# Seven block products for two of the mixer's column groups, in a four-layer decoder trunk

## The chip, the core and the metric

The kernel runs on one core of a Trainium2 chip. The metric is the device time of one execution in microseconds (us). The engines are TensorE (PE, with its weight loads as PEld), VectorE (DVE), ScalarE (ACT), GpSimd (POOL) and SyncE (SP), which issues the transfers from HBM. Each works through its own queue in order and waits for the others through semaphores.

## The reference

Four residual layers work on x of 256 tokens x 1024 features, all in float32:

```
for i in range(4):
    hn   = rmsnorm(x, g_mix[i])
    proj = hn @ w_in[i]                   # 1024 -> 3*1024 + 256
    cols, mq = proj[:, :3072], proj[:, 3072:]
    mix  = stick_breaking(cols)           # layers 1 and 4: q, k, v
         | diff_attention(cols, ...)      # layer 2:        q, k, v
         | b * conv3(c * h)               # layer 3:        b, c, h
    mo   = memory_attention(mq, rmsnorm(mem), w_mem_kv[i])
    x    = x + concat(mix, mo) @ w_o[i]
    x    = x + (silu(g) * u) @ w_ffn_out[i]   where g, u = rmsnorm(x) @ w_ffn_in[i]
out = rmsnorm(x, g_final)
```

The three 1024-wide parts of the mixer's projection are queries, keys and values in layers 1, 2 and 4, and the gates b, c and the input h in layer 3. The feed-forward part is 2816 wide.

## The kernel before

The tokens are two tiles of 128 (t = 0, 1); the 1024 features are eight chunks of 128 (kc). Every weight is split on the core into a high part that TensorE multiplies in its fast float32 form and a low part, weight minus high part; activations are split likewise. A product of activations and weights is then three matmuls (`mm3`, L135 to L138): high x high, high x low, low x high. `wparts` (L128) makes the two parts: a cast on ScalarE (`whi`, L131) and a subtraction on VectorE (`wlo`, L132), each for a chunk of 128 x 1024 numbers.

`proj` (L157) multiplies the tokens by one group of 512 weight columns: four chunks of two kc each, then, for each tile t, 8 x 3 matmuls of 128 x 512 into one PSUM bank, and an output function `evac(t, ps)`. The mixer works on two halves g = 0, 1 of the features: `mixer(g)` calls `proj` for 512 columns of q, of k and of v (in layer 3 of c, of h and of b). The transposes of the outputs, the attention and the convolution are put on a list with `later(n, f)` and are traced n flushes later; `proj` flushes in the middle and at the end of each token tile. So the small work of one group comes between the matmuls of the next ones. `memory()` (L716) projects the memory queries, 256 columns, and puts the cross-attention on the list.

`strassen` (L197) is a second way to do two column groups at once. It treats the tokens as a 2 x 2 matrix of blocks (token tile x half of the features) and the weights of the two groups as another (half of the features x group) and forms the product from seven block products instead of eight (Winograd's variant of Strassen's scheme). The products run in the order 1, 5, 7, 6 (each in two steps s of 256 features, the four of s = 0 before those of s = 1), then 2, 4 and 3. Their 14 weight chunks are made by eight sums of weight blocks on VectorE (`plus`, L224, 128 x 1024 each) and 14 calls of `wparts`. The sums `su` and `sy` of finished products are formed on VectorE, and `out(t, side, ps, add)` receives each of the four output blocks, three of them with an addition. Each of the seven products is 4 x 3 matmuls. `tokens_side` (L269) forms the sums of token blocks from the transposed inputs `xg`: four additions and four subtractions of 128 x 512 on VectorE, four casts on ScalarE. One group of outputs comes with its sign reversed, and `negative(rx)` gives the scale that puts it right.

Before the change the feed-forward part uses `strassen` for its column groups b = 1 and b = 4 (gate and up columns together), and straight `proj` calls for the other groups. `tokens_side` stands behind the first `proj` of b = 0.

The raw weights come from HBM on the SP queue into a pool of eight buffers (`wraw`), which also holds the weight sums. The parts stand in eight buffers each (`wsplit`). The output projection (`out_proj`, L293) keeps its last four chunks in `wsplit` until its end, where each of its four PSUM banks is finished in turn and handed to the residual addition, the norm's statistics and the transposes for the next stage. The transposed inputs `xg` stand in four buffers named `qkn`, which other work uses too; the split token blocks stand in a pool of eleven buffers named `att`.

Order on each engine: the kernel doesn't write it out. Instructions are traced in program order, and a planner puts them on the engines' queues by that order and by what is ready at its own reckoning, waiting for buffers where a pool is full. On the chip each queue is then strictly in order.

Of the kernel before, what the change touches and what calls it, by code (L numbers as in the profile page):

```python
# [9 lines left out]
F32 = mybir.dt.float32  # L10
# [7 lines left out]
P = 128  # L18
# [22 lines left out]
def trunk_kernel(ctx, tc, x, mem, vecs, w_in, w_kv, w_o, w_f1, w_f2, lams, g_final, out):  # L41
# [101 lines left out]
    def later(rounds, f):  # L143
        pend.append([rounds, f])
# [320 lines left out]
    def qkv_evac(dst, scale):  # L465
        def evac(t, ps):
            n = work.tile([P, 512], F32, name="qkn", tag="qkn", bufs=4)
            nc.scalar.activation(n, ps, AF.Copy, scale=scale[t])
            later(1, lambda: to_T(n, dst[:, :, t * P:(t + 1) * P], 1))
        return evac  # L470
# [231 lines left out]


    kv = None
    for i in range(DEPTH):
        kind = i % 3
        col = lambda c, n=512: [w_in[i, :, c:c + n]]
# [8 lines left out]
        def memory():  # L716
            mqT = big.tile([P, 2, 2, S], F32R, name="mqT", tag="big")

            def evac(t, ps):
                n = work.tile([P, MEMW], F32, name="mk", tag="att", bufs=NATT)  # L720
                nc.scalar.activation(n, ps[:, :MEMW], AF.Copy, scale=rx[t])
                later(1, lambda: queries(t, n))

            def queries(t, n):
                tr = ps_x.tile([P, 4, P], F32, name="tr", tag="ps")
                for c in range(2):
                    nc.tensor.transpose(tr[:, c, :], n[:, c * P:(c + 1) * P], ident)
                split(mqT, tr[:, :2, :], t)

            proj(col(3 * D, MEMW), xT, evac)  # L730
            later(2, lambda: om.append(mem_attention(mqT, kv)))

        rq = []

        def q_scale(t):
            r = small.tile([P, 1], F32, name="rq", tag="sm", bufs=14)
            nc.vector.tensor_scalar(r, rx[t], QSCALE, None, ALU.mult)
            return r
# [5 lines left out]
        if kind != 2:  # L744
            v = [big.tile([P, D], F32, name=f"v{t}", tag="big") for t in range(NT)]

            def mixer(g):
                qT = big.tile([P, 4, S], F32, name="qT", tag="big")
                kT = big.tile([P, 4, S], F32, name="kT", tag="big")
                sc = []  # L750

                def q_evac(t, ps):
                    if g == 0:
                        rq.append(q_scale(t))
                    qkv_evac(qT, rq)(t, ps)

                def scores():
                    if kind == 0:
                        sb_scores(qT, kT, sc, values)
                    else:  # L760
                        diff_scores(qT, kT, 2 * g, lam, sc, values)

                def v_evac(t, ps):
                    nc.scalar.activation(v[t][:, g * 512:(g + 1) * 512], ps, AF.Copy, scale=rx[t])

                def values():
                    outputs(g)
                    if kind == 0:
                        sb_values(sc, v, g * 512, oh[g], ol[g])
                    else:  # L770
                        diff_values(sc, v, g * 512, oh[g], ol[g], ghead)

                proj(col(g * 512), xT, q_evac, second_tile if i == 0 and g == 0 else None)
                if i > 0 and g == 0:
                    memory()
                if i == 0 and g == 0:
                    fetch_mem()
                proj(col(D + g * 512), xT, qkv_evac(kT, rx))
                if i == 0 and g == 0:
                    load_mem()  # L780
                later(2, scores)
                proj(col(2 * D + g * 512), xT, v_evac)
        else:
            def mixer(g):
                cn = [work.tile([P, 512], F32, name="cn", tag="qkn", bufs=4) for _ in range(NT)]
                uT = big.tile([P, 4, S], F32, name="uT", tag="big")
                bT = big.tile([P, 4, S], F32, name="bT", tag="big")

                def c_evac(t, ps):
                    nc.scalar.activation(cn[t], ps, AF.Copy, scale=rx[t])  # L790

                def h_evac(t, ps):
                    nc.vector.scalar_tensor_tensor(cn[t], ps, rx[t], cn[t], ALU.mult, ALU.mult)
                    later(1, lambda: to_T(cn[t], uT[:, :, t * P:(t + 1) * P], 1))

                def mix():
                    outputs(g)
                    conv_mix(bT, uT, oh[g], ol[g], g)

                proj(col(D + g * 512), xT, c_evac)  # L800
                if g == 0:
                    memory()
                proj(col(2 * D + g * 512), xT, h_evac)
                proj(col(g * 512), xT, qkv_evac(bT, rx))
                later(2, mix)

        mixer(0)
# [89 lines left out]
        def f_lhs(kc, t):  # L897
# [1 line left out]
            sl = slice(t * P, (t + 1) * P)  # L899
            return hh[:, kc % 4, sl], hl[:, kc % 4, sl]  # L900

        nxt, rnx = [], []
        out_proj(w_f2[i], list(range(NFF // 2)), f_lhs, 2,
                 residual(V_MIX + 8 * (i + 1), nxt, rnx) if i + 1 < DEPTH else final())
        xT, rx = nxt, rnx


# [28 lines left out]
```

## Time and profile before

| what | value |
|---|---|
| median of 3 runs | 1285.72 us (1285.38 to 1285.79) |
| the profiled execution | 1284.95 us |
| its span, first to last instruction | 1283.2 us |
| granted TensorE clock | 0.998 |
| busy: PE, PEld, DVE, ACT, POOL | 99%, 82%, 72%, 56%, 4% |
| weights read from HBM | 225 MB, 176 GB/s over the span |

Busy times are unions of the profiled instructions. Matmuls overlap one another, so the duration of one is longer than the distance between the starts of two, and a busy TensorE is not TensorE at its peak. A row of a group gives its count, its busy time and the mean duration of one; a row of waits gives the sum, the count and the longest. In a timeline the first two numbers are start and duration in us, and the bracket gives the idle time before the instruction and what ended it. Layers are counted from 1 in this text and from 0 in the code (i).

### The profile page before, as it was taken

What the parts mean: (1) busy time and instruction counts of PE and PEld (TensorE: products, weight loads), DVE (VectorE), ACT (ScalarE), POOL (GpSimd) and SP (SyncE); (2) the same over time, 40 slices, a digit from 0 to 9 for tenths busy, and PEclk for the clock granted to TensorE, in tenths of its full rate; (3) what the DMA queues carried; (4) which work ended last, traced back from release to release, by engine and by line L of the source; (5) the groups of instructions that cost most, each with busy time, mean ns of one, the idle gap of its engine ahead of it and who ended that gap; (6) DMA issues with size and microseconds to landing.
All of it is one profiled execution on the core that took longest, in us unless ns stands there. A gap on an engine that the chain in (4) does not pass through costs nothing.

```text
span 1283.2 us, 16324 instructions
## 1 busy us (share of the span) xinstructions
PE 1270.3 (99%) x6079; PEld 1046.2 (82%) x6079; DVE 923.2 (72%) x1147; ACT 721.4 (56%) x1015; POOL 55.0 (4%) x109
## 2 busy tenths in 40 slices
PE   9999999999999999999999999999999999999997
PEld 6888888878888888887888888887888888888786
DVE  7755599884566769988466778988646656998942
ACT  7756466564455646656355455656436755665642
POOL 1000000000111000000000000000000001000001
PEclk9999999999999999999999999999999999999999
DMA  9644438386554344848655553666765444383840
GB/s 347 199 145 134 145 115 279 116 290 206 149 184 131 132 148 122 272 131 291 191 158 164 173 190 105 200 202 200 244 195 165 132 132 148 103 279 110 270 156 33
DMA packets 107791, 227.34 MB, mean 177 GB/s; under 512 B 7488, under 2 KB 20288, under 8 KB 107712
## 3 DMA queue, kind: packets, MB, share of 16 engines
q1 hardware_dynamic: 107712, 226.31, 55.1%
q8 instruction: 47, 0.77, 0.2%
q14 instruction: 32, 0.26, 0.1%
HBM read 225.23 MB, written 1.05 MB: 176 GB/s over the span
## 4 chain that ended last, share of the span: by engine, by line
PE 91%; DVE 5%; ACT 1%; DMA 1%; issue 1%; SPq 0%; POOL 0%; POOLq 0%; ACTq 0%
PE acc L136 25%; PE acc L138 25%; PE acc L137 25%; PE acc L214 3%; DVE wlo L132 3%; PE acc L215 3%; PE acc L216 3%; PE tr L864 1%; PE tr L361 1%; PE tr L347 1%; DVE wsum L224 1%; ACT whi L131 1%; PE tr L430 1%; DMA raw<-in_w_ffn_out 1%; PE at L411 1%
## 5 line engine op out<-in xcount | busy, mean ns | idle before, releaser
L132 DVE TENSOR_TENSOR wlo<-raw,whi 128x1024 fp32r<-128x1024 f32 (+1 forms) x428 | 512.5, 1210 | 202.0 <-ACT whi L131 199.6
L131 ACT CAST whi<-raw 128x1024 fp32r<-128x1024 f32 (+1 forms) x428 | 438.8, 1042 | 291.0 <-PE acc L138 215.1
L136 PE MATMUL acc<-whi,xth 128*128 128x512 f32 (+1 forms) x896 | 353.5, 395 | 0.1
L137 PE MATMUL acc<-wlo,xth 128*128 128x512 f32 (+1 forms) x896 | 342.8, 383 | 1.6 <-DVE wlo L132 1.6
L138 PE MATMUL acc<-whi,xtl 128*128 128x512 f32 (+1 forms) x896 | 343.8, 384 | 0.0
L138 PEld LDWEIGHTS acc<-whi,xtl 128*128 128x128 f32 x896 | 168.4, 188 | 33.8
L137 PEld LDWEIGHTS acc<-wlo,xth 128*128 128x128 f32 x896 | 168.9, 188 | 32.6 <-DVE wlo L132 2.8
L136 PEld LDWEIGHTS acc<-whi,xth 128*128 128x128 f32 x896 | 168.6, 188 | 31.5 <-issue 0.8
L136 PE MATMUL acc<-whi,hh 128*128 128x512 f32 x320 | 125.4, 392 | 0.0
L138 PE MATMUL acc<-whi,hl 128*128 128x512 f32 x320 | 124.6, 389 | 0.0
L137 PE MATMUL acc<-wlo,hh 128*128 128x512 f32 x320 | 124.6, 389 | 0.0
L131 ACT CAST whi<-wsum 128x1024 fp32r<-128x1024 f32 x48 | 50.5, 1052 | 42.7 <-DVE wsum L224 39.2
L138 PEld LDWEIGHTS acc<-whi,hl 128*128 128x128 f32 x320 | 60.1, 188 | 12.6
L137 PEld LDWEIGHTS acc<-wlo,hh 128*128 128x128 f32 x320 | 60.1, 188 | 12.2
L136 PEld LDWEIGHTS acc<-whi,hh 128*128 128x128 f32 x320 | 60.1, 188 | 12.1
L132 DVE TENSOR_TENSOR wlo<-wsum,whi 128x1024 fp32r<-128x1024 f32 x48 | 58.4, 1217 | 5.8 <-ACT whi L131 5.2
L136 PE MATMUL acc<-whi,oh 128*128 128x512 f32 x128 | 51.1, 399 | 0.0
L214 PE MATMUL acc<-whi,sh 128*128 128x512 f32 x128 | 51.0, 399 | 0.0
L138 PE MATMUL acc<-whi,ol 128*128 128x512 f32 x128 | 50.0, 391 | 0.0
L216 PE MATMUL acc<-whi,sl 128*128 128x512 f32 x128 | 50.0, 390 | 0.0
L215 PE MATMUL acc<-wlo,sh 128*128 128x512 f32 x128 | 49.9, 390 | 0.0
L137 PE MATMUL acc<-wlo,oh 128*128 128x512 f32 x128 | 49.9, 390 | 0.0
(219 smaller groups left out, 1563.8 us busy)
## 6 DMA issues: line engine op xcount, KB each, us to landing
raw<-in_w_ffn_in SPq DMA_DIRECT2D x160, 512.0 KB, 4.5
raw<-in_w_in SPq DMA_DIRECT2D x100, 512.0 KB, 4.4
raw<-in_w_ffn_out SPq DMA_DIRECT2D x88, 512.0 KB, 4.6
raw<-in_w_o SPq DMA_DIRECT2D x40, 512.0 KB, 4.2
raw<-in_w_mem_kv SPq DMA_DIRECT2D x16, 512.0 KB, 4.4
raw<-in_w_ffn_in SPq DMA_DIRECT2D x32, 256.0 KB, 3.1
raw<-in_w_in SPq DMA_DIRECT2D x8, 256.0 KB, 5.6
x<-in_x SPq DMA_DIRECT2D x4, 256.0 KB, 4.2
```

Source lines behind the costliest of these rows:

```text
L131: nc.scalar.copy(hi, raw)
L132: wlast[:] = [nc.vector.tensor_tensor(lo, raw, hi.bitcast(F32), ALU.subtract)]
L136: nc.tensor.matmul(ps, lh, wh, start=first, stop=False)
L137: nc.tensor.matmul(ps, lh, wl, start=False, stop=False)
L138: return nc.tensor.matmul(ps, ll, wh, start=False, stop=last)
L214: nc.tensor.matmul(acc[b], lh[:, kc, :], w[0][:, k, :], start=start, stop=False, skip_group_check=True)
L215: nc.tensor.matmul(acc[b], lh[:, kc, :], w[1][:, k, :], start=False, stop=False, skip_group_check=True)
L216: nc.tensor.matmul(acc[b], ll[:, kc, :], w[0][:, k, :], start=False, stop=stop, skip_group_check=True)
L224: nc.vector.tensor_tensor(out, a, b, ALU.add)
L347: last_pe = nc.tensor.transpose(ps[:, c, :], src[:, kc * P:(kc + 1) * P], ident).ins
L361: nc.tensor.transpose(ps[:, c, :], src[:, c * P:(c + 1) * P], ident)
L411: nc.tensor.matmul(pss[r][:, pr, :], qT[r * 64:(r + 1) * 64, a, pr, t * P:(t + 1) * P], kT[r * 64:(r + 1) * 64, b, pr, :], start=a + b == ...
```

## The change

In layers 2 to 4 (i > 0) the first half (g = 0) of the mixer no longer does its three groups by three `proj` calls. In layers 2 and 4 the values' group comes first, by `proj`; queries and keys follow together by `strassen`; the memory queries come behind them, and the scores are put on the list ahead of the memory queries. In layer 3 the gate b comes first, then c and h by `strassen`, then the memory queries. The outputs go through `qk_out` (scale and transpose) and `ch_out` (scale, product, transpose). To feed `tokens_side`, the transposed inputs of the mixer are kept from the feed-forward part before (`xg_in`), and `tokens_later` puts `tokens_side` on the list, two flushes into the first `proj`. The second half g = 1 and layer 1 stay as they were.

```
+    xg_in = None
...
+        def tokens_later(xg=xg_in):
+            got = []
+            later(2, lambda: got.append(tokens_side(xg, xT)))
+            return got
...
+                def qk_out(t, side, ps, add):
+                    n = work.tile([P, 512], F32, name="qkn", tag="qkn", bufs=4)
+                    if add is not None:
+                        nc.vector.tensor_tensor(n, ps, add, ALU.add)
+                    nc.scalar.activation(n, ps if add is None else n, AF.Copy, scale=(rneg if side else rq)[t])
+                    later(1, lambda: to_T(n, (kT if side else qT)[:, :, t * P:(t + 1) * P], 1))
...
+                if i > 0 and g == 0:
+                    side = tokens_later()
+                    proj(col(2 * D), xT, v_evac)
+                    rq.extend(q_scale(t) for t in range(NT))
+                    rneg = negative(rx)
+                    strassen(col(0)[0], col(D)[0], side[0], qk_out)
+                    later(2, scores)
+                    memory()
+                    return
+
                 proj(col(g * 512), xT, q_evac, second_tile if i == 0 and g == 0 else None)
-                if i > 0 and g == 0:
-                    memory()
...
+                def ch_out(t, side, ps, add, got={}):
+                    src = ps
+                    if add is not None:
+                        src = cn[t] if side == 0 else add
+                        if (t, side) == (0, 1):
+                            src = work.tile([P, 512], F32, name="sx", tag="att", bufs=NATT)
+                        nc.vector.tensor_tensor(src, ps, add, ALU.add)
+                    if side == 0:
+                        nc.scalar.activation(cn[t], src, AF.Copy, scale=rx[t])
+                    got[t, side] = src
+                    if (t, 1 - side) in got:
+                        nc.vector.scalar_tensor_tensor(cn[t], got[t, 1], rneg[t], cn[t], ALU.mult, ALU.mult)
+                        later(1, lambda: to_T(cn[t], uT[:, :, t * P:(t + 1) * P], 1))
...
-                proj(col(D + g * 512), xT, c_evac)
                 if g == 0:
+                    side = tokens_later()
+                    proj(col(0), xT, qkv_evac(bT, rx))
+                    rneg = negative(rx)
+                    strassen(col(D)[0], col(2 * D)[0], side[0], ch_out)
                     memory()
-                proj(col(2 * D + g * 512), xT, h_evac)
-                proj(col(g * 512), xT, qkv_evac(bT, rx))
+                else:
+                    proj(col(D + g * 512), xT, c_evac)
+                    proj(col(2 * D + g * 512), xT, h_evac)
+                    proj(col(g * 512), xT, qkv_evac(bT, rx))
                 later(2, mix)
...
-        nxt, rnx = [], []
+        nxt, rnx, xg_in = [], [], []
         out_proj(w_f2[i], list(range(NFF // 2)), f_lhs, 2,
-                 residual(V_MIX + 8 * (i + 1), nxt, rnx) if i + 1 < DEPTH else final())
+                 residual(V_MIX + 8 * (i + 1), nxt, rnx, xg_in) if i + 1 < DEPTH else final())
```

## The prediction

> **What bounds the kernel now.** I read the head of the page first, then the chain that ended last, then who makes TensorE wait.
>
> ```profile
> span 1283.2 us, 16324 instructions
> PE 1270.3 (99%) x6079; PEld 1046.2 (82%) x6079; DVE 923.2 (72%) x1147; ACT 721.4 (56%) x1015; POOL 55.0 (4%) x109
> PE 91%; DVE 5%; ACT 1%; DMA 1%; issue 1%; SPq 0%; POOL 0%; POOLq 0%; ACTq 0%
> PE acc L214 <- DVE sy L224: 2.5, 4, 0.7
> PEld acc L214 <- DVE sy L224: 5.3, 8, 1.1
> ```
>
> TensorE is never idle for long and carries 91% of the chain, so a matmul taken away is worth its price as long as the other engines keep up. The only wait of TensorE that comes back in every layer lies inside the seven-product block itself (L214), which the kernel already uses twice in each feed-forward part. VectorE at 72% is an average, and the stages will turn out to differ.
>
> The price of a matmul is not its duration in the groups (0.39 us), since matmuls overlap. It is the distance from start to start. TensorE's timeline in the second feed-forward output projection:
>
> ```profile
> 299.78 0.39 PE L136 MATMUL acc<-whi,hh 128*128 128x512 f32 x1
> ...
> 336.95 0.39 PE L138 MATMUL acc<-whi,hb 128*128 128x512 f32 x1
> 337.19 0.60 PE L347 MATMUL tr<-ident,x 128*128 128x128 f32 x4
> 337.54 0.48 PE L136 MATMUL acc<-whi,hh 128*128 128x512 f32 x1
> ```
>
> From the first to the second row lie 164 steps: 37.17 / 164 = 0.2267 us a matmul. A group of four transposes takes 337.54 - 337.19 = 0.35 us.
>
> Now the stages of one layer by window (columns: length, busy time of each engine, clock, share of the DMA engines, GB/s):
>
> ```profile
> core 0: us, PE busy (x) PEld busy (x) DVE busy (x) ACT busy (x) POOL busy (x), PEclk, DMA share, GB/s
> 479.90:502.80 22.90, 22.90 (x108) 18.95 (x107) 22.41 (x29) 16.12 (x22) 0.75 (x2) 1.00 0.42 120
> 502.80:522.60 19.80, 19.80 (x89) 15.99 (x88) 19.77 (x22) 13.56 (x16) 0.00 (x0) 1.00 0.62 187
> 662.60:674.10 11.50, 11.50 (x56) 9.52 (x55) 9.70 (x13) 8.30 (x11) 1.82 (x2) 1.00 0.66 189
> 355.90:362.20 6.30, 6.30 (x55) 6.30 (x54) 3.33 (x4) 3.14 (x4) 0.00 (x0) 1.00 0.86 294
> 662.60:745.50 82.90, 82.47 (x431) 67.49 (x430) 62.62 (x104) 44.99 (x70) 1.82 (x2) 1.00 0.54 166
> ```
>
> The first row is the feed-forward part's first pair of column groups, done straight (two `proj`); the second is its next pair, done as seven products. The pair costs 22.9 less two transpose groups, 22.2 us; the seven products cost 19.8 less one, 19.45 us. So the same trick saves 2.7 us in a place where the trace shows it. But in both rows VectorE is full: 22.41 of 22.9 and 19.77 of 19.8. There the block has two straight projections ahead of it in which VectorE can run ahead. In the changed mixer it has one. That is the question of this change.
>
> **The change, part by part.** *Matmuls.* Two straight groups are 2 x 48 matmuls of 128x512, seven products are 7 x 4 x 3 = 84. Twelve fewer in each of three layers, 12 x 0.2267 = 2.72 us a layer, 8.2 us in all, all of it on the path. Transposes, memory queries (48 matmuls of 256 columns, the 6.30 us row) and weight transfers stay the same in number. The page "TensorE: Matmul & The Clock Gate" of the Trainium skill (section "Wait — 56ns, not 53.3ns?") puts warm 512-column matmuls 215.7 ns apart; this trace has 226.7. By the page the 36 matmuls would be 7.8 us, an estimate; the row decides.
>
> *VectorE.* Prices from its timeline:
>
> ```profile
> 333.03 1.23 DVE L132 TENSOR_TENSOR wlo<-raw,whi 128x1024 fp32r<-128x1024 f32 x1 [1.50 <-ACT whi L131]
> ...
> 342.86 1.23 DVE L132 TENSOR_TENSOR wlo<-raw,whi 128x1024 fp32r<-128x1024 f32 x1 [0.98 <-ACT whi L131]
> 344.00 0.68 DVE L355 TENSOR_TENSOR xtl<-xg,xth 128x512 fp32r<-128x512 f32 x1
> 344.61 0.68 DVE L351 TENSOR_TENSOR xg<-tr,vec 128x512 f32<-128x512 f32 x1
> ...
> 349.92 0.99 DVE L355 TENSOR_TENSOR xtl<-xg,xth 128x512 fp32r<-128x512 f32 x1
> ...
> 470.29 1.22 DVE L224 TENSOR_TENSOR wsum<-raw 128x1024 f32<-128x1024 f32 x1
> 472.21 1.23 DVE L224 TENSOR_TENSOR raw<-raw 128x1024 f32<-128x1024 f32 x1
> ...
> 488.26 1.22 DVE L224 TENSOR_TENSOR wsum<-raw 128x1024 f32<-128x1024 f32 x1
> ...
> 498.81 1.21 DVE L132 TENSOR_TENSOR wlo<-wsum,whi 128x1024 fp32r<-128x1024 f32 x1
> 499.94 1.22 DVE L132 TENSOR_TENSOR wlo<-raw,whi 128x1024 fp32r<-128x1024 f32 x1
> ```
>
> Back to back, a 128x1024 operation occupies VectorE for 499.94 - 498.81 = 1.13 us and a 128x512 one for 344.61 - 344.00 = 0.61 us. The change adds per layer six low-part splits (14 chunks in place of 8) and eight weight sums, 14 x 1.13 = 15.9; `tokens_side` with eight operations of 128x512, 4.8; the two partial results `su` and `sy` and three additions in the output function, 3.0. Together 23.7 us a layer, 71 us in all. VectorE's total goes from 923 to about 994 us, 78% of some 1280: not a bound overall, but it falls into one stretch.
>
> *ScalarE* adds six casts of weights, four of tokens and a copy, at most 11 x 0.96 = 10.6 us a layer by this row of its timeline (5.78 / 6 a cast; the last five are half as large). With 56% busy, and 13.56 of 19.8 us inside the present block, that stays hidden behind VectorE.
>
> ```profile
> 518.08 5.78 ACT L131 CAST whi<-raw 128x1024 fp32r<-128x1024 f32 x6
> ```
>
> *The running sum for VectorE.* Take layer 2, in which the first matmul of the input projection starts at 343.9. There are eight split buffers. Four hold the last chunks of the projection before, four the chunks of the values' projection, which are done by 334.2 (row 333.03). So the first split of the new block can run at 342.86, where the first tail buffer comes free. From 342.9 VectorE must do, up to the block's last (14th) chunk: what is left of the transposed inputs, six operations from 344.00 to 349.92, 3.6; `tokens_side`, 4.8; the small scales, 0.3; 14 splits, 15.9; the weight sums not done earlier; `su` and `sy`, 1.2; one output addition, 0.6; two copies of transposed queries and keys, 1.2. Of the eight sums two ran long before the block in the feed-forward case (470.29 and 472.21) and the third only at 488.26, when a raw buffer came free of the second straight projection. In the mixer no second projection holds raw buffers, so all four sums that need raw weights alone can run in VectorE's idle time before 342.9 (1.5 us before row 333.03). I take four early, four left: 4.5. Sum 32.1 us, so the 14th split ends at 375.0.
>
> TensorE without any wait: 343.9 + 11.5 (one straight projection with its transposes, row 662.60) + 13 chunks of 6 x 0.2267 = 17.7 + two transpose groups, 0.7 = 373.8. VectorE is 1.2 us late at the end. Walked chunk by chunk in program order, the block's first ten chunks are in time, the first of the fourth product comes 0.3 late and the second 1.4, because the two copies and a sum stand ahead of its split, and TensorE ends 1.8 late. I take 1.7: a layer then gains 2.72 - 1.7 = 1.0 us. The bounds: the present block's own loss, 19.45 - 84 x 0.2267 = 0.4 us, in which case it gains 2.3; and 1.8 + 2 x 1.13 = 4.1 us, if only two sums go early, in which case it loses 1.4.
>
> *What else moves.* The memory queries, their attention and the scores of the first half now start after the block, over the second half's three straight projections instead of the first half's two. Before the output projection reads them TensorE still has four straight projections to do, 4 x 48 x 0.2267 = 43.5 us, so that costs nothing unless VectorE is still behind. In layer 3 it may be: VectorE is busy for 62.62 of 82.9 us there, and with 23.7 more, less four early sums, it has 81.8 us of work in a stretch that TensorE would leave in 80.2. What is over has to come out of the lead it has in the memory keys and the output projection behind. I give that layer 0.5 us in place of 1.0.
>
> The masks and biases of layer 2 run on GpSimd while VectorE is full:
>
> ```profile
> 346.94 0.68 DVE L355 TENSOR_TENSOR xtl<-xg,xth 128x512 fp32r<-128x512 f32 x1
> 349.36 3.72 POOL L107 TENSOR_SCALAR abias<-dist 128x384 f32<-128x384 f32 x2
> 402.53 2.43 POOL L107 TENSOR_SCALAR abias<-dist 128x384 f32<-128x384 f32 x2
> ```
>
> Beside them one VectorE operation took 0.99 instead of 0.68 us (rows 349.92 and 346.94): 0.3 us, inside the 1.7. "SBUF — State Buffer" of the Trainium skill (section "Who interferes with whom") says that a VectorE instruction with two SBUF inputs and a GpSimd one that reads SBUF block each other for whole instructions. By that rule layer 2 could lose the 3.72 us of those two scalings, an estimate, and nearly all sums and splits are of that kind; the trace shows the slowdown mostly on GpSimd's side (3.72 against 2.43).
>
> **The sum.** 1.0 + 0.5 + 1.0 = 2.5 us off the profiled execution's own 1284.95 gives 1282.45. The median of the runs, 1285.72, lies 0.77 above that execution, so the forecast is 1283.2 us.
>
> **Rivals.** *Full gain.* The block loses only the 0.4 us that it loses in the feed-forward part: 3 x 2.3 = 6.9, 1278.8 us. For it: VectorE was full there too, and TensorE hardly noticed. Against: that block had 11 us more of straight matmuls before it. *Eaten up.* VectorE's backlog meets the attention chains, whose small operations TensorE needs in order, and each layer gives back its 1.0: 1285.5 us. For it: layer 3's balance. Against: at 99% VectorE the feed-forward stretch runs smoothly. *Slower.* The sums of the block's second half don't go early, because the raw buffers rotate as in the feed-forward part. From the running sum, each layer then waits 1.7 + 2.3 = 4.0 us for 2.72 saved, -1.3, and layer 3 -1.8: 4.4 us, and half of that if the backlog is partly caught: 1288 us. It decides at 342.9: if the third and fourth sum end behind the first split of the block, it is this case. That the change doesn't remove the matmuls is excluded by its loops.
>
> **How the numbers follow.** Forecast case 0.50, full gain 0.18, eaten up 0.14, slower 0.18. A measurement of this kernel can tell 0.2%, 2.6 us, from no change. The forecast lies on that line, so its half goes slightly to faster: 0.27 and 0.23. Faster 0.18 + 0.27 = 0.45; same 0.23 + 0.14 = 0.37; slower 0.18. The forecast case alone spans 1281.5 to 1285; the range reaches to the full gain, 1278.6, and to the slower case, 1288.
>
> **What would show it.** 36 fewer matmuls at L136 to L138 and L214 to L216 taken together. VectorE full from the values' projection to the block's end. The block's window 20.5 to 21.5 us long where the feed-forward's is 19.8, with TensorE waiting for `wlo` in its second half, above all at the fourth product. Four sums at L224 ahead of the first split of each mixer block. I am wrong if the mixer's block is as short as the feed-forward's, if waits at the attention's transposes grow by more than 1 us a layer, or if the sums run late.

## The result, and the profile after

| | before | after |
|---|---|---|
| median | 1285.72 us | 1305.43 us (4 runs, 1305.24 to 1305.84) |
| ratio | | 1.0154, 95% interval 1.0137 to 1.0172 |
| the profiled execution, its span | 1284.95, 1283.2 us | 1305.24, 1303.5 us |

The changed kernel is 1.5% slower: 19.7 us, where 2.5 us less were forecast. From the page of the changed kernel, its head and the shares of the chain that ended last:

```profile
span 1303.5 us, 16376 instructions
...
PE 1273.7 (98%) x6043; PEld 1045.0 (80%) x6043; DVE 992.8 (76%) x1234; ACT 745.4 (57%) x1048; POOL 58.1 (4%) x109
...
PE 78%; DVE 12%; ACT 4%; DMA 2%; issue 2%; POOL 1%; SPq 0%; POOLq 0%; ACTq 0%; DVEq 0%
```

The 36 matmuls are gone (6079 to 6043) and VectorE has the 70 us more that were worked out (923.2 to 992.8). But TensorE is busy for 3.4 us *more*, and stands still for 29.8 us instead of 12.9 (span less busy time). In the chain VectorE's share has gone from 5% to 12%.

Where the time went is read by stage. The three mixers of layers 2 to 4, from the first matmul of the input projection to the first of the output projection (columns as in the prediction: window, length, busy time of each engine, granted clock, share of the DMA engines, GB/s), before:

```profile
343.90:451.10 107.20, 107.20 (x569) 89.31 (x568) 76.16 (x140) 64.87 (x136) 15.13 (x28) 1.00 0.47 148
662.60:757.20 94.60, 94.17 (x486) 77.07 (x485) 71.79 (x119) 51.97 (x81) 1.82 (x2) 1.00 0.54 168
968.70:1059.90 91.20, 91.20 (x491) 76.19 (x489) 56.37 (x85) 58.03 (x100) 5.07 (x11) 1.00 0.49 151
```

and after:

```profile
344.10:456.10 112.00, 107.69 (x556) 88.02 (x555) 94.79 (x165) 73.25 (x147) 16.82 (x28) 0.98 0.47 152
667.60:772.70 105.10, 96.27 (x473) 77.93 (x472) 89.97 (x143) 59.74 (x92) 1.06 (x2) 0.95 0.50 161
984.20:1080.20 96.00, 91.77 (x478) 75.17 (x477) 75.30 (x109) 65.70 (x111) 7.05 (x11) 0.98 0.49 154
```

They are longer by 4.8, 10.5 and 4.8 us, 20.1 of the span's 20.3: the whole loss lies in them. TensorE's idle time in them (length less busy time) went from 0, 0.4 and 0 us to 4.3, 8.8 and 4.2, 17.4 in all. And the clock column is no longer 1.00. What TensorE waited for, after (sum, times, longest, in us):

```profile
PE tr L430 <- DVE mprob L422: 6.0, 4, 3.5
PE tr L361 <- DVE cn L824: 2.9, 1, 2.9
PE tr L361 <- ACT qkn L773: 2.8, 2, 1.6
PE acc L214 <- DVE sy L224: 2.5, 4, 0.7
PE at L494 <- ACT sb_uh L487: 1.9, 1, 1.9
PE tr L564 <- DVE df_p L556: 1.5, 1, 1.5
...
PE acc L137 <- DVE wlo L132: 1.1, 2, 0.8
PE tr L361 <- ACT qkn L468: 1.0, 1, 1.0
PE acc L215 <- DVE wlo L132: 0.7, 2, 0.5
```

The wait for `wlo` inside the block, on which the prediction spent its running sum, is 0.7 us (L215) as far as it shows as idle time. The large ones are transposes and small matmuls: of the memory attention (L430), of the block's outputs (L361), of the two kinds of scores (L494, L564). In the profile of before only the first of these is there, once, beside the feed-forward's (L214, L137):

```profile
PE tr L430 <- DVE mprob L422: 0.4, 1, 0.4
```

**The clock.** Windows of the changed kernel ahead of and after each fall of the granted clock (its column stands behind the POOL one):

```profile
395.20:398.60 3.40, 2.25 (x17) 1.67 (x18) 3.40 (x7) 0.87 (x3) 0.00 (x0) 1.00 0.82 275
398.60:402.00 3.40, 3.40 (x10) 2.61 (x9) 1.79 (x6) 1.19 (x2) 0.00 (x0) 0.50 0.99 319
723.00:726.30 3.30, 2.04 (x16) 1.36 (x16) 2.79 (x10) 3.30 (x8) 0.00 (x0) 1.00 0.36 142
726.30:729.70 3.40, 3.40 (x17) 2.69 (x14) 3.40 (x11) 2.14 (x5) 0.00 (x0) 0.50 0.00 0
733.10:736.50 3.40, 1.05 (x5) 0.55 (x3) 2.64 (x6) 1.02 (x4) 0.00 (x0) 1.00 0.45 154
736.50:743.30 6.80, 5.62 (x18) 4.78 (x19) 2.67 (x7) 1.79 (x3) 0.00 (x0) 0.50 0.42 154
1033.50:1036.90 3.40, 2.13 (x18) 1.46 (x18) 1.26 (x3) 1.84 (x4) 0.57 (x1) 1.00 0.78 251
1036.90:1040.30 3.40, 3.40 (x10) 2.75 (x9) 1.52 (x5) 0.44 (x1) 0.00 (x0) 0.50 0.14 57
```

Apart from the start and the end of the execution, the clock falls to half four times, for 3.4, 3.4, 6.8 and 3.4 us: 17.0 us. Each time TensorE had been busy for only 31 to 66% of the 3.4 us ahead. "TensorE: Matmul & The Clock Gate" of the Trainium skill (section "What's actually happening") gives half rate after an idle window of about 3.4 us, windows that run on by themselves. The trace agrees on the length, and on the grid: from fall to fall lie 327.7, 10.2 and 300.4 us, 96.0, 3.0 and 88.0 times 3.413. It differs on the idleness, of which more at the end.

**The account.** Of the 17.0 us at half speed TensorE was busy for 3.40 + 3.40 + 5.62 + 3.40 = 15.8 us, so half speed adds at most 7.9 us that aren't idle time already. Minus 8.2 (36 matmuls), plus 17.4 - 0.4 idle, plus 7.9 is 16.7 us of the 20.1 in the three windows. That half speed counts in full isn't shown. The mean granted clocks of the four executions are 0.992, 0.994, 0.994 and 0.993; the second and third thus have about 4 us or more less at half speed than the first, which is the profiled one, and with 1305.84 and 1305.29 us they are no faster than its 1305.24. Of the other 3.4 us, 1.8 lie inside the blocks of layers 2 and 4, about 0.9 in each (their 83 steps from one full matmul to the next took 20.1 us, those of the feed-forward's first block 19.2). Where a low part comes late there, the step to the next matmul takes 0.47 us in place of 0.23, but the matmul before it lasts 0.39 us and covers most of the gap, so it counts as busy:

```profile
368.57 0.39 PE L214 MATMUL acc<-whi,xth 128*128 128x512 f32 x1
369.04 0.50 PE L215 MATMUL acc<-wlo,xth 128*128 128x512 f32 x1
```

The rest, about 1.6 us, is not placed.

**What stands ahead of the waiting transposes.** VectorE in layer 3 before the longest wait (timeline: start, duration, then in the bracket the idle time before and what ended it), and the transposes:

```profile
734.19 0.75 DVE L828 SCALAR_TENSOR_TENSOR cn<-acc,rstd,cn 128x512 f32<-128x512 f32 x1 [0.76 <-PE acc L138]
734.85 1.22 DVE L132 TENSOR_TENSOR wlo<-raw,whi 128x1024 fp32r<-128x1024 f32 x1
735.99 0.17 DVE L420 RECIPROCAL msm<-msm 128x4 f32<-128x4 f32 x1
736.07 1.20 DVE L132 TENSOR_TENSOR wlo<-raw,whi 128x1024 fp32r<-128x1024 f32 x1
737.19 1.14 DVE L422 TENSOR_SCALAR mprob<-mprob,msm 128x256 f32<-128x256 f32 x4
```

```profile
737.68 1.94 PE L430 MATMUL tr<-ident,mprob 128*128 128x128 f32 x8 [3.53 <-DVE mprob L422]
```

The softmax's reciprocal and scaling stand in VectorE's queue among an output and two weight splits; before these rows, the memory's first token tile stands among the convolution's operations. At the block's end it is the same with ScalarE, here in layer 3:

```profile
699.97 1.05 ACT L131 CAST whi<-raw 128x1024 fp32r<-128x1024 f32 x1 [1.39 <-DMA raw<-in_w_in]
701.29 1.05 ACT L131 CAST whi<-raw 128x1024 fp32r<-128x1024 f32 x1 [0.27 <-DMA raw<-in_w_in]
702.24 0.72 ACT L821 ACTIVATE cn<-cn,rstd 128x512 f32<-128x512 f32 x1
```

```profile
700.47 0.39 PE L216 MATMUL acc<-whi,sl 128*128 128x512 f32 x1
703.80 0.66 PE L361 MATMUL tr<-ident,cn 128*128 128x128 f32 x4 [2.95 <-DVE cn L824]
```

The block's last matmul starts at 700.47. One of its last outputs, which VectorE had added up by 700.65 (L819), is scaled by ScalarE only at 702.24, behind casts for the *next* projection, one of which waited 1.39 us for raw weights. Then VectorE multiplies (L824), and TensorE, whose next item is the transpose of that output, waits 2.95 us with the memory queries' matmuls queued behind it.

### The profile page after: what moved, and what is told of

Its sections match the earlier page's. It is cut to its first block, busy times and chain, and to the rows that moved or that the text cites. A ratio compares the mean times of both kernels' runs of the same rounds, so it can differ in the third digit from the quotient of the medians.

```text
span 1303.5 us, 16376 instructions
## 1 busy us (share of the span) xinstructions
PE 1273.7 (98%) x6043; PEld 1045.0 (80%) x6043; DVE 992.8 (76%) x1234; ACT 745.4 (57%) x1048; POOL 58.1 (4%) x109
## 4 chain that ended last, share of the span: by engine, by line
PE 78%; DVE 12%; ACT 4%; DMA 2%; issue 2%; POOL 1%; SPq 0%; POOLq 0%; ACTq 0%; DVEq 0%
PE acc L136 21%; PE acc L138 21%; PE acc L137 21%; DVE wlo L132 6%; PE acc L214 3%; PE acc L216 3%; PE acc L215 3%; ACT whi L131 2%; DMA raw<-in_w_in 1%; DVE wsum L224 1%; PE tr L904 1%; PE tr L347 1%; PE tr L361 1%; DMA raw<-in_w_ffn_out 1%; ACT mprob L418 1%
## 5 line engine op out<-in xcount | busy, mean ns | idle before, releaser
L136 PE MATMUL acc<-whi,xth 128*128 128x512 f32 (+1 forms) x800 | 316.9, 396 | 0.6 <-ACT xth L354 0.6
L137 PE MATMUL acc<-wlo,xth 128*128 128x512 f32 (+1 forms) x800 | 307.5, 385 | 1.1 <-DVE wlo L132 1.1
L138 PE MATMUL acc<-whi,xtl 128*128 128x512 f32 (+1 forms) x800 | 308.3, 386 | 0.0
L137 PEld LDWEIGHTS acc<-wlo,xth 128*128 128x128 f32 x800 | 152.4, 191 | 29.2 <-DVE wlo L132 2.2
L137 PE MATMUL acc<-wlo,hh 128*128 128x512 f32 x320 | 124.6, 389 | 0.0
L131 ACT CAST whi<-wsum 128x1024 fp32r<-128x1024 f32 x66 | 69.4, 1052 | 59.8 <-DVE wsum L224 56.2
L132 DVE TENSOR_TENSOR wlo<-wsum,whi 128x1024 fp32r<-128x1024 f32 x66 | 80.4, 1219 | 6.4 <-ACT whi L131 5.8
L214 PE MATMUL acc<-whi,sh 128*128 128x512 f32 x176 | 70.1, 398 | 0.0
L137 PEld LDWEIGHTS acc<-wlo,hh 128*128 128x128 f32 x320 | 60.1, 188 | 12.2
L215 PE MATMUL acc<-wlo,sh 128*128 128x512 f32 x176 | 68.9, 391 | 0.0
L214 PE MATMUL acc<-whi,xth 128*128 128x512 f32 x132 | 52.5, 398 | 2.5 <-DVE sy L224 2.5
L224 DVE TENSOR_TENSOR wsum<-wsum,raw 128x1024 f32<-128x1024 f32 x44 | 53.1, 1219 | 0.3
L215 PE MATMUL acc<-wlo,xth 128*128 128x512 f32 x132 | 52.3, 396 | 1.0 <-DVE wlo L132 0.7
```

Source lines behind the costliest of these rows:

```text
L131: nc.scalar.copy(hi, raw)
L132: wlast[:] = [nc.vector.tensor_tensor(lo, raw, hi.bitcast(F32), ALU.subtract)]
L136: nc.tensor.matmul(ps, lh, wh, start=first, stop=False)
L137: nc.tensor.matmul(ps, lh, wl, start=False, stop=False)
L138: return nc.tensor.matmul(ps, ll, wh, start=False, stop=last)
L214: nc.tensor.matmul(acc[b], lh[:, kc, :], w[0][:, k, :], start=start, stop=False, skip_group_check=True)
```

## The experiments

The times of 1 to 8 are of one execution each, beside one of the kernel before on the same chip; the others are medians, with an interval for the ratio. Lengths of blocks and idle times are of the three mixers in order; a block's length runs from its first to its last matmul. The 23.5 us that some expectations give for the changed kernel's block reach on to the transposes behind it (680.7 to 704.2 in layer 3). `later(n, f)` puts f on the list n flushes ahead.

**1. The order alone.** Values (or b) first and the memory queries last, as in the change, but straight projections throughout and no token sums.

```
-                    strassen(col(0)[0], col(D)[0], side[0], qk_out)
+                    proj(col(0), xT, qkv_evac(qT, rq))
+                    proj(col(D), xT, qkv_evac(kT, rx))
...
-                    strassen(col(D)[0], col(2 * D)[0], side[0], ch_out)
+                    proj(col(D), xT, c_evac)
+                    proj(col(2 * D), xT, h_evac)
```

> The new order of the column groups alone, in layers 2 to 4: values (or b) first, then the two other groups straight by proj, then the memory queries; no seven products, no token sums. Theory L (load: the sums, splits and token blocks in one stretch make VectorE and ScalarE late, and TensorE waits for them): 1285 to 1288 us, no drop of the granted clock, the waits at the transposes of the mixer as in the kernel before. Theory O (order: memory attention, scores and convolution mix now fall together over the second half): at least half of the 20 us stays, 1295 us or more, with the waits at the transposes of the probabilities (L430) in layer 3.

Measured: 1295.54 us, before 1286.07. Without a block product in the mixers, the order alone costs 9.5 us. That is theory O, though not only in layer 3: from its input projection to the end of its output projection, layer 3 is 6.5 us longer than before, layers 2 and 4 are 1.9 and 1.7. The clock fell once, at 731.8. Layer 3 in a window of this kernel, and what TensorE waits for in it:

```profile
720.00:730.00 10.00, 7.62 (x42) 5.71 (x40) 10.00 (x25) 5.92 (x17) 0.00 (x0) 1.00 0.03 4
```

```profile
PE tr L430 <- DVE mprob L422: 6.7, 4, 4.2
```

VectorE is full for these 10 us, TensorE is busy for 7.62 of them: the memory attention, put behind the first half's third group, meets the first half's mixing and the second half's weight splits.

**2. Without the weight sums.** The eight sums on VectorE are left out of the mixers' blocks; where a sum makes a new buffer (two of the eight), ScalarE copies one of its terms there.

```
+        def wplus(out, a, b, fresh=False):
+            if sums_on:
+                plus(out, a, b)
+            elif fresh:
+                nc.scalar.copy(out, a)
...
-            plus(b12, b12, b22[s])
+            wplus(b12, b12, b22[s])
```

> The changed kernel with the eight weight sums of each mixer block left out (the two fresh sum tiles are filled by a ScalarE copy, so buffers and casts stay): VectorE has 9 us a layer less, ScalarE 2 more; the mixer's numbers are not the reference's. Theory L: the block falls from 23.5 to about 20 us in each layer, the waits behind it shrink too, 1278 to 1288 us. Theory O: the block gets shorter, but the waits of the second half and the half clock stay: 1292 to 1298 us.

Measured: 1295.43 us, before 1286.07. That is in the range of theory O, but the block, which both theories had shorter, hardly is (21.3, 20.2 and 21.2 us against 21.7, 20.0 and 21.4). With 9 us of VectorE work a layer 10 us of the loss go, elsewhere: the wait at L494 is gone, and the falls of the clock went from four to two; L430's wait is 6.7 us. The 9.4 us that stay are as much as the order alone cost.

**3. More straight work ahead.** The second half's queries (in layer 3 its b) projected before the block as well.

```
+                    ahead.append(big.tile([P, 4, S], F32, name="qT", tag="big"))
+                    proj(col(512), xT, qkv_evac(ahead[0], rq))
                     strassen(col(0)[0], col(D)[0], side[0], qk_out)
```

> The changed kernel with a second straight projection ahead of the block (queries, in layer 3 gate b, of the second half), so the block has two in front as in the feed-forward part, and the second half has one less behind. Theory L: VectorE can run ahead, the block takes about 20 us in place of 23.5, 1280 to 1292 us. Theory O: the second half is shorter for the same attention work: no better than 1300 us.

Measured: 1296.30 us, before 1286.07; blocks 21.4, 19.7 and 21.1 us. It lies between the two theories, and not by the mechanism of either: a second projection in which VectorE can run ahead shortens the blocks by 0.3 us each, and L430's wait is 6.7 us here too. What is 9 us better than in the changed kernel lies in other waits (L494 is gone) and in two falls of the clock instead of four.

**4. The output transposes later.**

```
-                    later(1, lambda: to_T(n, (kT if side else qT)[:, :, t * P:(t + 1) * P], 1))
+                    later(2, lambda: to_T(n, (kT if side else qT)[:, :, t * P:(t + 1) * P], 1))
```

and so in `ch_out`, with scores and mixing one flush later too.

> The changed kernel with the transposes of the block's outputs, and the scores or mix behind them, put one flush later on the list. If TensorE's waits of 1.6, 2.9 and 1.2 us at the end of the three blocks are only a matter of the place of these transposes in TensorE's queue, they vanish and 5 to 9 us come back: 1296 to 1300 us. If the lateness is just handed on to the next wait (the memory projection's weights, the scores): 1303 to 1306 us.

Measured: 1295.46 us, before 1286.07. 10 us are gained, a little more than the first case gave, but the waits that were to vanish did not: those at L361 for `qkn` (L773) are 4.0 us, more than the changed kernel's 2.8, and only layer 3's for `cn` is gone. L430 keeps 5.7. Gone as well are the waits at L494 and L564 (1.9 and 1.5 us): a shift of one flush moves other collisions too.

**5 and 6. Scores and mixing spread out,** in the kernel with the order alone and in the changed kernel:

```
-                    later(2, scores)
+                    later(8, scores)
...
-                later(2, mix)
+                later(2 if g else 10, mix)
```

> The new order of the groups without the seven products, as in order_only, but the scores of the first half are put six flushes later on the list and the convolution mix eight, so that they no longer fall on the memory attention. Theory C (collision: in the new order the memory attention shares VectorE with the scores or the mix, and TensorE waits behind it at the transposes of the probabilities): layer 3 falls from 101.1 to about 95 us, the clock stays at 1.0, 1286 to 1288 us in all. If the new order costs for another reason (memory attention merely too late): 1293 us or more.

> The changed kernel with the scores and the mix put later in the same way. Theory C and a separate loss at the block's end that adds to it: 1305.4 less the 7 to 9 us of order_only that the spreading gets back, 1296 to 1298 us. If the block's lateness is what makes the collision: 1303 us or more, as the block stays.

Measured: 1287.26 and 1292.11 us, before 1285.19. The order's loss shrinks from 9.5 to 2.1 us, the changed kernel's from 19.7 to 6.9, with the computation unchanged. What TensorE still waits for in the second:

```profile
PE tr L361 <- DVE cn L824: 3.5, 1, 3.5
PE tr L361 <- ACT qkn L773: 2.8, 2, 1.5
...
PE tr L430 <- DVE mprob L422: 1.0, 1, 1.0
```

L430 has fallen from 6.0 to 1.0 us. So most of the loss was the collision of the small work. The changed kernel came out better than either case expected. The rest, 1292.11 - 1287.26 = 4.9 us, is the block itself, and nearly all of it lies in layer 3, whose mixer takes 98.9 us against 94.9 in 5. With the 8.2 us that it should have saved the block costs 13: waits at its ends (L361, 6.3 us), one fall of the clock at 700.4 (1.7 us at most), and, by an estimate that is worked out below for the changed kernel, some 4 us of delays inside the blocks.

**7. The memory queries ahead of the block,** their attention held back till behind it (nine flushes), and scores and mixing spread over 6 and 10.

```
+                    memory(9)
...
                     strassen(col(0)[0], col(D)[0], side[0], qk_out)
-                    later(2, scores)
-                    memory()
+                    later(6, scores)
```

> The changed kernel with the memory queries' projection moved in front of the block (behind the values or gate b), its attention still behind the block, scores and mix later as in after_spread. The block has 16.8 us of straight matmuls ahead instead of 10.9, and what follows it are 512-column chunks, not the memory queries' weights. If lead is what the block lacks: block near 20.5 us, 1286 to 1292 us. If not: like after_spread, within 2 us.

Measured: 1289.17 us, before 1285.19; idle 1.5, 4.5 and 1.4 us, no fall of the clock, blocks 21.1, 19.6 and 21.1 us. 2.9 us better than 6, in the range expected if lead were what the block lacks; but the blocks are only 0.3 to 0.4 us shorter than in 6 (21.4, 20.0 and 21.4), so lead is a small part of it.

**8. Scaling on VectorE** of the outputs that have an addition, in place of ScalarE, in the changed kernel; in `ch_out` likewise.

```
-                    nc.scalar.activation(n, ps if add is None else n, AF.Copy, scale=(rneg if side else rq)[t])
+                    if add is None:
+                        nc.scalar.activation(n, ps, AF.Copy, scale=rq[t])
+                    else:
+                        nc.vector.tensor_scalar(n, n, (rneg if side else rq)[t], None, ALU.mult)
```

> The changed kernel with the scaling of the block's three outputs that have an addition done on VectorE right behind the addition, not on ScalarE. Theory S (at the block's end the scaling stands in ScalarE's queue behind casts that wait for weights from HBM): TensorE's waits of 1.6, 2.9 and 1.2 us at the output transposes fall below 0.7 each, and with fewer drops of the clock 5 to 9 us come back: 1296 to 1300 us. If VectorE's own backlog makes them late: no gain, 1303 to 1307 us.

Measured: 1302.80 us, before 1285.19. 2.6 us better than the changed kernel, just outside the range of "no gain" and far from theory S. The waits at L361 behind the block fell from 5.7 to 3.9 us. ScalarE's queue at the block's end is a part of it, a small one beside the collisions.

**9. Memory queries ahead and output transposes later** (7 and 4 together).

> The kernel with the memory queries ahead of the block (1289.2 us), and the transposes of the block's outputs one step later. Theory (what is left at the block's end is the wait of the output transposes, 1.7 to 2.0 us at L361 in each layer, behind VectorE's and ScalarE's queues): those waits fall below 0.5 us, TensorE's idle time in the three mixers goes from 7.4 to some 3 us, and the time to 1285 to 1286. Rival (VectorE owes the work anyway, and the wait only moves to the next operation that needs it, the transposes of the attention at L430 or the following projection): idle time stays at 6 us or more, 1288 to 1290.

Measured: 1285.05 us, before 1285.27; ratio 0.9999, interval 0.9989 to 1.0009. The theory's time came: the loss is gone. The idle time fell from 7.4 to 5.0 us, less far than expected; the wait for `cn` vanished, those for `qkn` (1.7 at L468, 1.6 at L773) stayed. Another 1.3 us, in 7 as in 9, lies in layer 4's output projection, into which its attention now reaches.

**10. As 7, without the weight sums** (left out as in 2).

> The kernel with the memory queries ahead of the block, without the eight sums of weights in each mixer block (9.0 us of VectorE a layer; the products are then formed from unsummed weights, so that the output isn't the reference's). Theory (VectorE's backlog makes the block 21.1 us long and late at its end): the block falls to 19.5 to 20 us and the waits at L361 to under 1 us, 1289.2 - 3 x (1.4 + 1.0) = 1282, that is faster than the kernel before by 3 us: the matmuls saved do count once VectorE keeps up. Rival (the ends of the block wait for ScalarE and raw weights, not for VectorE): 1287 or more.

Measured: 1285.00 us, before 1285.27; ratio 0.9998, interval 0.9989 to 1.0008. Between the two expectations: 4.2 us better than 7. The waits at the outputs' transposes fall from 5.6 to 3.8 us, but the blocks stay at 21.3, 20.4 and 21.3 us. So the sums do not set the length of the block; since two copies take their place on ScalarE, the run doesn't settle what does.

**11. Both the memory queries and the second half's query group ahead,** transposes later. Scores and mixing are back at two and three flushes here (6 and 10 in 9), the memory attention at eleven (nine in 9).

> The kernel with the memory queries and the later transposes, and with the straight projection of the second half's queries (the second half of b in layer 3) ahead of the block as well, so that two straight groups and the memory queries stand in front of it. Theory (VectorE needs that much straight work to run ahead, as in the feed-forward part): blocks of 20 us or less and 1282 to 1285, better than both kernels. Rival (the second half then has only two projections over which the attention of the first half, the memory's and the scores can spread; they collide again): waits at L430 of 3 us or more in a layer come back and the time is 1288 or more.

Measured: 1292.48 us, before 1285.27; ratio 1.0058, interval 1.0043 to 1.0073. This is the rival's time, and its kind of wait (L564 2.5 us, L430 2.8 us in all, not 3 in a layer); the blocks gain little (20.9, 19.7, 20.7). Whether the second half with two projections is too short, or the scores and the mixing merely stood too close again, the run doesn't separate.

**12. As 9, with two left-over waits treated:** in layer 3 the memory queries before b, in layer 4 the scores three flushes earlier.

```
-                    later(6, scores)
+                    later(3 if kind == 0 else 6, scores)
...
+                    memory(11)
                     proj(col(0), xT, qkv_evac(bT, rx))
-                    memory(9)
```

> The kernel with the memory queries ahead and the later transposes (1285.05 us, the same as the kernel before), with two of its left-over waits treated: in layer 3 the memory queries come before the straight projection of b, so that b's outputs find their buffers free (a wait of 1.7 us at L361 for ScalarE's L468), and in layer 4 the scores of the first half start three steps earlier, so that their chain doesn't reach into the output projection (waits of 0.9 us for oh and of 0.4 us at L494 there). Theory (the twelve matmuls a layer do count once TensorE's own waits are gone): 1285.05 - 1.7 - 1.3 = 1282, faster than the kernel before by some 3 us. Rival (VectorE is the bound in these stretches, and a wait removed comes back behind the next operation): 1284.5 or more.

Measured: 1289.76 us, before 1285.22; ratio 1.0036, interval 1.0022 to 1.0050. It lies in the rival's range: a wait removed came back behind the next operation, and three times as long. Layer 3 is worse by this one wait, and the clock falls behind it.

```profile
PE tr L728 <- ACT mk L722: 5.1, 1, 5.1
```

```profile
676.10:679.50 3.40, 0.00 (x0) 0.00 (x0) 3.40 (x5) 1.71 (x4) 0.00 (x0) 1.00 0.00 0
679.50:682.90 3.40, 3.27 (x9) 2.70 (x10) 2.25 (x4) 0.45 (x2) 0.00 (x0) 0.50 0.00 0
```

The memory queries' outputs now wait for ScalarE while VectorE is full, where b's had waited 1.7 us: who comes first at the head of this stage waits. Layer 4's edit did help, so it was run alone.

**13 and 14. As 9 with layer 4's scores earlier, and with layer 3's transposes of b later too.** 13 has the first edit of 12 alone; 14 has this one beside it:

```
-                    proj(col(0), xT, qkv_evac(bT, rx))
+                    proj(col(0), xT, qkv_evac(bT, rx, 2))
```

> The kernel with the memory queries ahead and the later transposes (1285.05 us), and in layer 4 alone the scores of the first half three steps earlier. Layer 4, from the start of its input projection to the end of its output projection, took 127.4 us in the former and 126.0 us in the kernel that also had the memory queries first in layer 3. Theory: 1285.05 - 1.4 = 1283.6. Rival (the layer gives it back after the output projection): 1285.

> As the kernel before it in this list, and in layer 3 the transposes of the straight projection of b one step later, since TensorE waited 1.7 us there for outputs that stand behind the four token sums (VectorE) and their casts (ScalarE). Theory (the matmuls that the seven products save come through once TensorE's own waits go): 1283.6 - 1.5 = 1282.1, faster than the kernel before by 0.2%. Rival (VectorE bounds that stretch, so that the wait comes back at the block or at the memory's transposes): 1283 to 1285.

Measured: 1283.47 and 1283.57 us, before 1285.46; ratios 0.9986 (0.9977 to 0.9995) and 0.9984 (0.9975 to 0.9992). 13 came out as its theory said. 14 lies in its rival's range but says nothing on its question: the transposes that wait stand at the same place of TensorE's queue, with the same wait of 1.68 us, and only those of the second token tile moved. The mixers of 13, for comparison with the two tables above:

```profile
343.90:450.10 106.20, 105.05 (x558) 87.09 (x557) 95.76 (x167) 72.56 (x147) 15.43 (x28) 1.00 0.49 155
661.50:755.30 93.80, 91.61 (x474) 74.85 (x473) 91.40 (x145) 58.86 (x92) 0.74 (x2) 1.00 0.55 175
966.80:1058.20 91.40, 89.28 (x479) 73.94 (x477) 77.66 (x111) 66.44 (x113) 6.70 (x12) 1.00 0.51 164
```

TensorE's busy time is 2 to 3 us less in each than before: the twelve matmuls a layer are there. Against it stand 1.2, 2.2 and 2.1 us of idle time. The layers win 1.0, 0.8 and lose 0.2 us. In layer 3 VectorE is busy for 91.4 of 93.8 us; before it was 71.8 of 94.6.

## Why the prediction was wrong

*Matmuls.* Right: 36 fewer, and where the waits are gone, TensorE's busy time shows them (13 against before: 2.1 + 2.6 + 1.9 = 6.6 us less in the three windows).

*The running sum.* Right in layers 2 and 4, too high in layer 3. In layer 2 the four sums ran early and the 14th split ended at 375.9 (forecast 375.0); VectorE of the changed kernel, the first and fourth sum, the first and 14th split:

```profile
323.51 1.22 DVE L224 TENSOR_TENSOR wsum<-raw 128x1024 f32<-128x1024 f32 x1
...
336.40 1.23 DVE L224 TENSOR_TENSOR raw<-raw 128x1024 f32<-128x1024 f32 x1 [0.18 <-DMA raw<-in_w_in]
...
342.96 1.23 DVE L132 TENSOR_TENSOR wlo<-raw,whi 128x1024 fp32r<-128x1024 f32 x1 [0.66 <-ACT whi L131]
...
374.71 1.21 DVE L132 TENSOR_TENSOR wlo<-raw,whi 128x1024 fp32r<-128x1024 f32 x1
```

The blocks took 21.7, 20.0 and 21.4 us from first to last matmul, where 20.5 to 21.5 were forecast. Less 84 x 0.2267 us and the transposes in them (two groups, one and two, of 0.35 us) they lost 2.0, 0.6 and 1.7 us; the forecast was 1.7 in each. The yardstick was kind: the 19.8 us are the feed-forward's first block, and its second one takes 20.7. Beside GpSimd's scalings in layer 2 VectorE lost the 0.3 us that were allowed for (the split at 365.73 took 1.52 us in place of 1.22). The *slower* rival, sums that run late, is refuted by these rows, and in layers 3 and 4 the four early sums lie ahead of the first split too: its sign came true by another mechanism.

*What failed is the step "What else moves".* It costed the moved memory queries, their attention and the scores at nothing, since 43.5 us of straight projections still followed before the output projection needs them, "unless VectorE is still behind", and charged 0.5 us in layer 3. That cover is for the *last reader*. But each transpose and small matmul of these chains has a fixed place in TensorE's queue between the projections' matmuls, and if its operand is late, TensorE stands there whatever may follow: 3.53 us at 737.68, with the next projection's matmuls behind it. The order alone cost 9.5 us (1), spread out 2.1 (5). The price of the move should have been the lateness of each small operation behind VectorE's other work: 0.5 to 3.5 us each at L430 in the changed kernel. (In layer 4 the cover is also one projection shorter than the sum has it, since no memory keys for a next layer follow: 32.6 us.)

*What was left out.* The block's end: the running sum stops at the last matmul of the block. The outputs then go through ScalarE and VectorE to a transpose that is TensorE's next item; that cost 2.9 us in layer 3 and 2.8 in layers 2 and 4 together (waits at L361). The prediction had ScalarE's added work hidden behind VectorE; at these ends it isn't. And the clock: the sum has no term for a stretch at half speed behind a wait; up to 7.9 us here.

*The rival "eaten up"* named the mechanism ("VectorE's backlog meets the attention chains, whose small operations TensorE needs in order") and bounded it at the gain, 1.0 us a layer, so at no change in the end; the mixers became 4.8 to 10.5 us longer. Its argument against, that the feed-forward stretch runs smoothly with a full VectorE, was no argument here: no attention crosses that block. The list of signs in the prediction had "waits at the attention's transposes grow by more than 1 us a layer" as what would make it wrong, and this is what came: 5.6 us more at L430 and 1.5 at L564, most of it in layer 3.

*That the cause is where the small work stands, and not the block products as such,* is shown by 1, 2, 6 and 13. The order without the products costs 9.5 us (1), the order with the products but without their sums on VectorE 9.4 (2): so the order makes about half of the 19.7, and the load of the sums in that order the other half. Moved apart, order and load cost nothing: the same products with their whole load, in another order of the small work, take 1283.47 us, 22 less (13). That VectorE's added work takes the rest of the 8.2 us is argued from its 91.4 of 93.8 us in layer 3; in layers 2 and 4 it isn't full, and which of its waits could still go stays open (10 didn't settle it, 14 didn't move what it meant to move).

## What to carry to other kernels

A matmul taken away counts only if every small operation that TensorE must run in order still has its operand in time: when work is added to VectorE or a chain is moved, walk through TensorE's queue item by item and ask for each transpose when its input leaves VectorE's and ScalarE's queues, rather than when its last reader needs it. Where a stage becomes full on VectorE, spread the attention's and the memory's chains over the projections (here `later` by 3 to 10 in place of 2) and don't put an output's transpose straight behind the block that makes it. A trial of the new order without the new arithmetic costs one run and would have shown half of the loss.

## What the runs showed of the hardware

The granted clock fell to half behind a stretch that was *not* wholly idle. Ahead of the fall at 726.3 TensorE did this:

```profile
722.82 0.39 PE L138 MATMUL acc<-whi,xtl 128*128 128x512 f32 x1
724.47 0.87 PE L430 MATMUL tr<-ident,mprob 128*128 128x128 f32 x6 [1.26 <-DVE mprob L422]
725.27 0.38 PE L411 MATMUL at<-mkT,mqT 64*128 64x256 f32 x1
725.58 0.44 PE L430 MATMUL tr<-ident,mprob 128*128 128x128 f32 x2
725.95 0.76 PE L411 MATMUL at<-mkT,mqT 64*128 64x256 f32 x6
```

The wait is 1.26 us; nearly all the rest of the 3.4 us are transposes and matmuls of 64 rows. In the windows ahead of 398.6 and 1036.9 it is a similar mixture, with waits of 1.5 and 1.9 us; ahead of 736.5 it is 1 us of full matmuls and then the wait. So a wait shorter than the window can cost the clock, for 3.4 us or more. It need not: run 7 had waits of 1.9 and 1.7 us between full matmuls (L361) and no fall, and the kernel of run 1 has the very sequence shown above, at 718.1, with a wait of 1.22 us and TensorE busy for 2.18 of 3.4 us, and kept its clock there.

Counted back from the falls on the grid of 3.413 us, in all the traces and with the falls at the ends of the executions, 29 of 32 falls come behind a window in which TensorE was busy for less than 1.47 us (43% of it), and no window as idle as that, begun at full clock, was without one. The other three are those of the changed kernel at 398.6, 726.3 and 1036.9, behind windows with 2.0 to 2.3 us; some thirty windows between 1.47 us and that had none. What sets the three apart is open. That transposes count little for the clock could be a part of it. "TensorE: Matmul & The Clock Gate" of the Trainium skill (section "Part 4: PE-mode transpose") says that they don't count as busy in the same way. No run here separates them from the waits, and run 11 kept its clock behind a window, at 403.5, of nothing but transposes and small matmuls, with TensorE busy for 2.06 of 3.41 us.
